# Keys and b/a from the input without its norm factor, with the factor applied at their evacuation; GpSimd makes the sums of squares and the normalized input

## The chip, the cores and the metric

One core of one Trainium2 chip runs the whole program. The metric is the device time of one execution in microseconds, the median of several runs. The engines are TensorE (PE in the profile, with its weight loads as PEld), VectorE (DVE), ScalarE (ACT), GpSimd (POOL) and SyncE (SP, which here only issues DMAs).

## The reference, cut to what matters

Two blocks of a sequence model on 256 positions of width 1024. The change touches only the very beginning, the first layer's input projections:

```python
def rmsnorm(x, w):
    y = x * lax.rsqrt(jnp.mean(x * x, axis=-1, keepdims=True) + EPS)
    return y * w

# gated_deltanet(hn = rmsnorm(x, a_norm_w))
proj = hn @ w_in                                   # 1024 -> q 1024, k 1024, v 2048, z 2048, b 16, a 16
qkv, z, b, a = split(proj)
qkv = silu(causal_dwconv(qkv, conv_w))             # four taps along the positions
q, k = l2norm(q) * 128 ** -0.5, l2norm(k)          # per head
beta, g = sigmoid(b), -exp(a_log) * softplus(a + dt_bias)
o = chunked_gated_delta_rule(q, k, v, g, beta)     # then norm, gate with z, output projection
```

The norm factor is one number per position, so `hn @ w` is `((x * a_norm_w) @ w)` times that factor.
After this layer follow a convolutional MLP, sliding-window attention, a second MLP, and a second block (gated linear attention beside latent attention, and an MLP).

## The kernel before

The activations are held transposed: 8 tiles of 128 channels by 256 positions (`self.h`). Every weight matrix is cut into 128x128 blocks. Eight blocks that are used one after the other lie together as a weight tile of 128x1024 floats (512 KB) in one long array `wall`, in the order of use. `_raw` (line 168) loads a tile through SP's queue. `_prep` (line 175) makes of it a high half `wh` on ScalarE (a copy that rounds, line 186) and a low half `wl` on VectorE (the rest, line 187). Raw tiles and halves have four buffers each. `w` (line 230) hands out the next block and prepares tiles up to two ahead. The input is split in the same way into `xh` and `xl`, and a product is three matmuls (`mm3`, line 247): wh times xh, wh times xl, wl times xh.

`gemm` (line 257) goes over column tiles of the output. With `ko=2` its first four column tiles run together with the channel index k outermost, so that each k needs only one tile of x: this is how Keys start. The others take all eight k for one column tile, one weight tile each.

The program is written in one order, with side tasks that take a step at every fourth block (`side`, `tick`). A scheduler then fixes each engine's own order by the order of writing and by when it reckons operands to be ready; `behind` (line 192) forces one instruction behind another on an engine. At run time each engine executes its list in order and waits with semaphores.

The start (`gdn`, line 547): x is loaded in four quarters ahead of the weights, the identity and the table of small columns. ScalarE squares the quarters, VectorE adds them (line 502) and folds them (line 558), TensorE sums over the channels (`colsum`, line 361), VectorE makes the reciprocal root (`rstd`, `rsqrt_k`, lines 370 and 341), and `rows` (line 410) spreads it over all partitions by a diagonal and a product with ones. Matmuls on ones (`warm`) fill some of the waits. Then for each of the 8 tiles VectorE multiplies x by norm weight and factor (line 568), ScalarE makes `xh` (line 569), VectorE `xl` (line 570).

In `gdn_body` (line 576) Keys' first group runs, then b/a (`w_ba`, evacuated by `evac_ba`, line 605), the rest of Keys, and then Queries, Values and gate z mixed. The evacuation of Keys and Queries is a four-tap convolution (`conv`, line 642): a scaled copy on ScalarE, three multiply-adds on VectorE for each column tile (line 650), a silu, and later sums of squares on TensorE (line 669). Many short-lived tiles share one pool of six buffers (tag `t2`): the normalized x (`xn`), the convolution's `cy`, b/a's `gr` and `gcr`, and others.

## Time and profile before

| | |
|---|---|
| median of 3 runs | 1217.02 us (1215.78 to 1218.51) |
| profiled execution | 1216.23 us, span 1214.4 us |
| TensorE busy | 1188.7 us, 98% |
| VectorE busy | 895.2 us, 74% |
| ScalarE busy | 687.7 us, 57% |
| GpSimd busy | 20.4 us, 2% |
| DMA | 206 MB, 170 GB/s on average |

The profile comes from one execution, on which the times of single instructions rest. Busy is the share of the span in which an engine executes; matmuls are pipelined, so that one of them is recorded longer than the distance to the next. A row of a timeline gives the start, the length, the engine, the line in the program, the operation, what it writes and reads, the shape, and how many like it were merged; in brackets stands how long the engine was idle before it and what released it.

### The profile page before, as it was taken

The page shows a single profiled execution, that of the slowest core. Times are in us where ns is not written, and L with a number is a line of the kernel's source. Part 1 is how long each engine was busy: PE and PEld are TensorE (multiplying, and loading weights), DVE is VectorE, ACT ScalarE, POOL GpSimd, SP SyncE. Part 2 cuts the span into 40 slices and gives each one's busy share as a digit, 9 for nine tenths or more (in the row PEclk, how much of TensorE's full clock was granted, in tenths as well). Part 3 has the DMA queues.
Part 4 walks back from the last instruction along what each step waited for, and adds up shares of the span by engine and source line. Part 5 has one row for each costly group of instructions (what it writes and reads, how often), then busy time and mean ns, then how long its engine had stood idle before and what let it go on. Part 6 is the DMA issues. An engine that isn't in the chain of part 4 may idle for free.

```text
span 1214.4 us, 23416 instructions
## 1 busy us (share of the span) xinstructions
PE 1188.7 (98%) x9368; PEld 1125.4 (93%) x9368; DVE 895.2 (74%) x1680; ACT 687.7 (57%) x1170; POOL 20.4 (2%) x47
## 2 busy tenths in 40 slices
PE   7999989999999999999999999999999999999997
PEld 6989878999999999889999999889789999999996
DVE  6978976668877778878977778756756567655555
ACT  5785547546655556656755556754465445444443
POOL 1000000000000000000000000000000000000000
PEclk9999999999999999999999999999999999999999
DMA  6546365355555557435555564364255563555552
GB/s 222 179 132 216 125 192 183 124 157 168 199 184 182 187 179 243 126 115 161 190 188 183 187 191 158 112 207 134 87 161 173 188 234 118 186 179 187 189 179 83
DMA packets 68318, 206.01 MB, mean 170 GB/s; under 512 B 18198, under 2 KB 18342, under 8 KB 67953
## 3 DMA queue, kind: packets, MB, share of 16 engines
q1 hardware_dynamic: 65600, 194.77, 50.3%
q0 software_dynamic: 2608, 9.75, 2.2%
q8 instruction: 73, 1.20, 0.4%
q14 instruction: 37, 0.29, 0.1%
HBM read 199.75 MB, written 4.74 MB: 168 GB/s over the span
## 4 chain that ended last, share of the span: by engine, by line
PE 92%; DVE 4%; ACT 2%; DMA 1%; issue 1%; SPq 0%; DVEq 0%; ACTq 0%
PE pb L249 21%; PE pb L250 20%; PE pb L251 20%; PE acc L249 7%; PE acc L250 7%; PE acc L251 7%; DVE wl L187 1%; PE pt L1138 1%; PE ssb L669 1%; DMA wr<-wall 0%; DMA h<-xT 0%; PE z2p L855 0%; PE y2p L847 0%; PE kv L1542 0%; PE csum L366 0%
## 5 line engine op out<-in xcount | busy, mean ns | idle before, releaser
L187 DVE TENSOR_TENSOR wl<-wr,wh 128x1024 fp32r<-128x1024 f32 x362 | 441.5, 1223 | 193.7 <-ACT wh L186 192.3
L186 ACT ACTIVATE wh<-wr 128x1024 fp32r<-128x1024 f32 x362 | 381.6, 1057 | 338.3 <-issue 101.1
L251 PE MATMUL pb<-xh,wl 128*128 128x256 f32 x1224 | 345.6, 283 | 3.9 <-DVE wl L187 3.9
L249 PE MATMUL pb<-xh,wh 128*128 128x256 f32 x1224 | 347.8, 284 | 0.6 <-ACT xh L569 0.6
L250 PE MATMUL pb<-xl,wh 128*128 128x256 f32 x1224 | 345.5, 282 | 0.2 <-DVE xl L570 0.2
L249 PEld LDWEIGHTS pb<-xh,wh 128*128 128x128 f32 x1224 | 231.7, 189 | 2.8 <-issue 1.3
L251 PEld LDWEIGHTS pb<-xh,wl 128*128 128x128 f32 x1224 | 229.7, 188 | 4.5 <-DVE wl L187 4.5
L250 PEld LDWEIGHTS pb<-xl,wh 128*128 128x128 f32 x1224 | 230.1, 188 | 0.5 <-DVE xl L570 0.4
L249 PE MATMUL pb<-fh,wh 128*128 128x256 f32 x416 | 118.3, 285 | 0.0
L250 PE MATMUL pb<-fl,wh 128*128 128x256 f32 x416 | 117.5, 283 | 0.1
L251 PE MATMUL pb<-fh,wl 128*128 128x256 f32 x416 | 116.6, 281 | 0.0
L249 PE MATMUL acc<-ah,wh 128*128 128x256 f32 x352 | 98.7, 280 | 0.0
L251 PE MATMUL acc<-ah,wl 128*128 128x256 f32 x352 | 98.5, 280 | 0.0
L250 PE MATMUL acc<-al,wh 128*128 128x256 f32 x352 | 98.5, 280 | 0.0
L249 PEld LDWEIGHTS pb<-fh,wh 128*128 128x128 f32 x416 | 77.9, 188 | 1.4 <-issue 0.4
L250 PEld LDWEIGHTS pb<-fl,wh 128*128 128x128 f32 x416 | 78.1, 188 | 1.1 <-DVE fl L436 0.3
L251 PEld LDWEIGHTS pb<-fh,wl 128*128 128x128 f32 x416 | 78.9, 190 | 0.0
L977 DVE SCALAR_TENSOR_TENSOR fy<-fpad,cols,fy 128x256 f32<-128x256 f32 x176 | 73.6, 478 | 0.0
L249 PE MATMUL pb<-wh,xh 128*128 128x512 f32 (+1 forms) x176 | 70.5, 402 | 0.0
L250 PE MATMUL pb<-wl,xh 128*128 128x512 f32 (+1 forms) x176 | 68.1, 387 | 0.5 <-DVE wl L187 0.5
L251 PE MATMUL pb<-wh,xl 128*128 128x512 f32 (+1 forms) x176 | 68.0, 387 | 0.0
L249 PEld LDWEIGHTS acc<-ah,wh 128*128 128x128 f32 x352 | 66.9, 190 | 0.0
(437 smaller groups left out, 2091.2 us busy)
## 6 DMA issues: line engine op xcount, KB each, us to landing
wr<-wall SPq DMA_DIRECT2D x362, 512.0 KB, 3.6
wzd<-zt POOLq DMA_DIRECT2D x8, 256.0 KB, 3.0
wzog<-wzd POOLq DMA_DIRECT2D x4, 512.0 KB, 5.2
bias<-bd POOLq DMA_DIRECT2D x4, 512.0 KB, 7.7
h<-xT SPq DMA_DIRECT2D x4, 256.0 KB, 4.0
h<-xT POOLq DMA_DIRECT2D x1, 1024.0 KB, 5.9
wrow<-wrow POOLq DMA_DIRECT2D x1, 1024.0 KB, 10.0
out_dram<-mw SPq DMA_DIRECT2D x4, 256.0 KB, 2.0
```

Source lines behind the costliest of these rows:

```text
L186: nc.scalar.activation(hi, r, AF.Copy)
L187: i = nc.vector.tensor_tensor(lo, r, hi.bitcast(F32), ALU.subtract)
L249: mm(out, ah, bh, start=start, stop=False, skip_group_check=skip)
L250: mm(out, ah, bl, start=False, stop=False, skip_group_check=skip)
L251: mm(out, al, bh, start=False, stop=stop, skip_group_check=skip)
L669: nc.tensor.matmul(ssb[:, c : c + 1], sq[:, i, tt * P : tt * P + P], self.ones[:, 0:1], start=True, stop=True)
L977: nc.vector.scalar_tensor_tensor(y[:, i], u[:, i, j : j + T], w(j), y[:, i], ALU.mult, ALU.add)
L1138: nc.tensor.transpose(pt[:, j * P : j * P + P], S[:, i, j * P : j * P + P], self.ident)
```

## The change

x times the norm weight alone is split into `raw` halves, and Keys and b/a are computed from these. Keys' evacuation multiplies by the factor (line 657 of before), and so does that of b/a. The normalized x, which Queries, Values and z still read, is made by a side task on GpSimd and ScalarE. The quarters of x and the first three weight tiles are loaded in turn; the identity goes through GpSimd's queue and the norm weights, by themselves, through ScalarE's. The first conversions stand in a written order on ScalarE and VectorE. Two of the additions of squares and one half of the folding move to GpSimd. In the k-outer products all wh times xh of one k come first, then wh times xl, then wl times xh. Three small products on VectorE are forced behind other work.

```diff
-WARM = (5, 1, 3)
+WARM = 16
+NA1, NA2 = 4, 2
@@ gemm, ko
             for k in range(K):
+                ts = []
                 for g in range(ko):
                     for i, c in enumerate(groups[g]):
-                        wh, wl = self.w(name, k * P, c * P)
-                        self.mm3(banks[g][:, i * T : i * T + T], wh, wl, xh[:, k], xl[:, k],
-                                 k == 0 and i == 0, k == K - 1, True)
+                        ts.append((banks[g][:, i * T : i * T + T], *self.w(name, k * P, c * P), k == 0 and i == 0))
+                mm = self.nc.tensor.matmul
+                for o, wh, wl, first in ts:
+                    mm(o, wh, xh[:, k], start=first, stop=False, skip_group_check=True)
+                for o, wh, wl, first in ts:
+                    mm(o, wh, xl[:, k], start=False, stop=False, skip_group_check=True)
+                for o, wh, wl, first in ts:
+                    mm(o, wl, xh[:, k], start=False, stop=k == K - 1, skip_group_check=True)
@@ run
+            self.ones = self.cp.tile([P, P], F32, name="ones")
+            nc.gpsimd.memset(self.ones, 1.0)
+            self.anw = self.cp.tile([P, KD], F32, name="anw")
+            nc.scalar.dma_start(self.anw, self.a["cols"][:, 0:KD])
             for b in range(4):
                 nc.sync.dma_start(self.h[:, 2 * b : 2 * b + 2], self.a["xT"][:, 2 * b : 2 * b + 2])
-            nc.sync.dma_start(self.ident, self.cst("ident"))
-            self._raw(0)
+                if b < 3:
+                    self._raw(b)
+            nc.gpsimd.dma_start(self.ident, self.cst("ident"))
             nc.sync.dma_start(self.cols, self.a["cols"])
@@ gdn (all of the old chain goes)
-            warm(WARM[0], self.ones)
-            for b in range(4):
-                self.add_sq(self.sqs, "sqa", b, lambda o: nc.scalar.activation(o, self.h[:, 2 * b : 2 * b + 2], AF.Square))
-            nc.vector.tensor_tensor(self.sqs[0], self.sqs[0], self.sqs[1], ALU.add)
-            cs = self.colsum(self.sqs[:1])
...
-            rc = self.rstd(cs, D)
...
-            rb = self.rows(rc, psum=True)
...
-            for i in range(8):
-                t = gp.tile([P, T], F32, tag="t2", bufs=6, name="xn")
-                op = nc.vector.scalar_tensor_tensor(t, self.h[:, i], self.col("a_norm", i), rb, ALU.mult, ALU.mult)
-                nc.scalar.activation(x[0][:, i], t, AF.Copy)
-                nc.vector.tensor_tensor(x[1][:, i], t, x[0][:, i].bitcast(F32), ALU.subtract)
...
+            for _ in range(WARM):
+                nc.tensor.matmul(wb[:, 0:P], self.ones, self.ones, start=True, stop=True)
+            raw = (gp.tile([P, KD, T], F32R, tag="XA", name="rawh"), gp.tile([P, KD, T], F32R, tag="EA", name="rawl"))
...
+            def rawtile(i):
+                act.append(nc.scalar.activation(raw[0][:, i], self.h[:, i], AF.Copy, scale=self.anw[:, i : i + 1]))
+                dve.append(nc.vector.scalar_tensor_tensor(raw[1][:, i], self.h[:, i], self.anw[:, i : i + 1], raw[0][:, i].bitcast(F32), ALU.mult, ALU.subtract))
+            def part(j, s):
+                r, hi, lo = self.raws0[j], *self.halves[j]
+                act.append(nc.scalar.activation(hi[:, s], r[:, s], AF.Copy))
+                dve.append(nc.vector.tensor_tensor(lo[:, s], r[:, s], hi[:, s].bitcast(F32), ALU.subtract))
+            def square(b):
+                t = gp.tile([P, 2, T], F32, tag="t2", bufs=6, name="sq")
+                act.append(nc.scalar.activation(t, self.h[:, 2 * b : 2 * b + 2], AF.Square))
+                return t
...
+            rawtile(0)
+            part(0, lo)
+            rawtile(1)
+            part(0, hi)
+            rawtile(2)
+            rawtile(3)
+            part(1, full)
+            s0 = square(0)
+            rawtile(4)
+            rawtile(5)
+            s1_ = square(1)
+            self._raw(3)
+            nc.gpsimd.tensor_tensor(s0, s0, s1_, ALU.add)
+            part(2, full)
+            s2_ = square(2)
+            nc.gpsimd.tensor_tensor(s0, s0, s2_, ALU.add)
+            rawtile(6)
+            rawtile(7)
+            s3_ = square(3)
+            self._raw(4)
+            nc.gpsimd.tensor_tensor(s0[:, 0], s0[:, 0], s0[:, 1], ALU.add)
+            dve.append(nc.vector.tensor_tensor(s3_[:, 0], s3_[:, 0], s3_[:, 1], ALU.add))
+            for l in (act, dve):
+                for p, n in zip(l, l[1:]):
+                    self.behind(n, p)
...
+            def norm():
+                for _ in range(NA1):
+                    yield
+                rc = self.rstd(self.colsum([s0[:, 0], s3_[:, 0]]), D)
+                for _ in range(NA2):
+                    yield
+                self.rb = self.rows(rc)
+                self.ready = True
+                self.flush()
+                for i in range(8):
+                    t = gp.tile([P, T], F32, tag="t2", bufs=6, name="xn")
+                    nc.gpsimd.tensor_tensor(t, self.ha[i], self.rb, ALU.mult)
+                    nc.scalar.activation(x[0][:, i], t, AF.Copy)
+                    nc.gpsimd.tensor_tensor(x[1][:, i], t, x[0][:, i].bitcast(F32), ALU.subtract)
+                    yield
...
+            for i in range(8):
+                nc.gpsimd.tensor_tensor(self.ha[i], self.h[:, i], self.anw[:, i : i + 1].to_broadcast([P, T]), ALU.mult)
+            self.side(norm())
@@ evac_ba
-            nc.vector.tensor_scalar(xa[A], b[A, :T], ...)
+            nc.vector.tensor_tensor(e1[A], b[A, :T], self.rb[A], ALU.mult)
+            nc.vector.tensor_scalar(xa[A], e1[A], ...)
@@ mk_evac
+                if key == "kss":
+                    u = t2([P, 2, T], "ku")
+                    nc.vector.tensor_tensor(u, ev2(b), self.bc2(self.rb), ALU.mult)
+                    b = u.rearrange("p a t -> p (a t)")
                 conv(b, ct0 + 2 * g, d)
@@ Keys and b/a
-        gk = self.gemm("w_in", x, KD, list(range(8, 16)), mk_evac(kT, 0, 8, "kss"), ko=2)
+        gk = self.gemm("w_in", raw, KD, list(range(8, 16)), mk_evac(kT, 0, 8, "kss"), ko=2)
         next(gk)
-        list(self.gemm("w_ba", x, KD, [0], evac_ba))
+        list(self.gemm("w_ba", raw, KD, [0], evac_ba))
@@ identr, and in ffn the two products wfp and w1f
+            self.behind(nc.vector.tensor_tensor(...), ...)
```

## Rows read from the trace of the kernel before

**Rows 1.** The page's busy time by engine: us, share of the span, instructions.
```profile
PE 1188.7 (98%) x9368; PEld 1125.4 (93%) x9368; DVE 895.2 (74%) x1680; ACT 687.7 (57%) x1170; POOL 20.4 (2%) x47
```
**Rows 2.** Busy time by stretches; first the view's own column names.
```profile
core 0: us, PE busy (x) PEld busy (x) DVE busy (x) ACT busy (x) POOL busy (x), PEclk, DMA share, GB/s
0.00:15.00 15.00, 7.46 (x26) 5.68 (x26) 6.71 (x25) 7.62 (x11) 1.36 (x9) 1.00 0.75 269
...
28.00:40.00 12.00, 12.00 (x102) 12.00 (x101) 10.99 (x24) 10.55 (x17) 0.00 (x0) 1.00 0.62 209
40.00:52.00 12.00, 12.00 (x104) 12.00 (x103) 11.94 (x22) 8.59 (x13) 0.00 (x0) 1.00 0.45 140
...
240.00:480.00 240.00, 239.84 (x2004) 238.41 (x2003) 192.27 (x322) 140.35 (x223) 4.79 (x10) 1.00 0.57 182
```
**Rows 3.** Timeline of TensorE, first 16 us; a matmul of f32 is recorded as two.
```profile
0.99 2.50 PE L554 MATMUL warm<-ones 128*128 128x128 f32 x10 [0.99 <-POOL ones L524]
9.29 1.01 PE L366 MATMUL csum<-ones,sqa 128*128 128x1 f32 x4 [5.80 <-DVE sqa L558]
15.02 0.50 PE L249 MATMUL pb<-xh,wh 128*128 128x256 f32 x2 [0.59 <-ACT xh L569]
```
**Rows 4.** Timeline of ScalarE, 4 to 62 us.
```profile
4.11 0.63 ACT L557 ACTIVATE sqa<-h 128x512 f32<-128x512 f32 x1 [2.10 <-DMA h<-xT]
...
8.43 1.06 ACT L186 ACTIVATE wh<-wr 128x1024 fp32r<-128x1024 f32 x1 [1.23 <-DMA wr<-wall]
...
10.45 1.06 ACT L186 ACTIVATE wh<-wr 128x1024 fp32r<-128x1024 f32 x1 [0.74 <-DMA wr<-wall]
...
16.22 1.01 ACT L569 ACTIVATE xh<-xn 128x256 fp32r<-128x256 f32 x3
...
28.62 0.46 ACT L647 ACTIVATE cy<-pb,cols 128x256 f32<-128x256 f32 x1
...
50.23 1.06 ACT L186 ACTIVATE wh<-wr 128x1024 fp32r<-128x1024 f32 x1 [0.85 <-PE pb L250]
```
**Rows 5.** Timeline of TensorE, two matmuls in a row and a block of sums.
```profile
24.06 0.28 PE L250 MATMUL pb<-xl,wh 128*128 128x256 f32 x1
24.18 0.28 PE L251 MATMUL pb<-xh,wl 128*128 128x256 f32 x1
...
46.01 0.95 PE L669 MATMUL ssb<-ones,sqg 128*128 128x1 f32 x8
```
**Rows 6.** Timeline of VectorE, 5 to 49 us; merged rows overlap a little.
```profile
5.81 0.69 DVE L502 TENSOR_TENSOR sqa<-sqa,sq 128x512 f32<-128x512 f32 x1 [5.81 <-ACT sq L557]
...
10.34 0.16 DVE L379 TENSOR_SCALAR rv<-csum 128x2 f32<-128x2 f32 x1 [1.11 <-PE csum L366]
...
12.93 0.48 DVE L416 TENSOR_SCALAR dg<-ident,rd 128x128 f32<-128x128 f32 x2
...
15.22 0.75 DVE L570 TENSOR_TENSOR xl<-xn,xh 128x256 fp32r<-128x256 f32 x2
...
18.82 1.26 DVE L568 SCALAR_TENSOR_TENSOR xn<-h,cols,rowp 128x256 f32<-128x256 f32 x3
...
28.75 1.23 DVE L187 TENSOR_TENSOR wl<-wr,wh 128x1024 fp32r<-128x1024 f32 x1 [2.52 <-ACT wh L186]
...
41.47 2.43 DVE L650 SCALAR_TENSOR_TENSOR cy<-pb,cols,cy 128x255 f32<-128x255 f32 x6
...
47.13 1.21 DVE L187 TENSOR_TENSOR wl<-wr,wh 128x1024 fp32r<-128x1024 f32 x1
```
**Rows 7.** A cast on GpSimd, VectorE beside it; line 187's shortest, median, longest in ns.
```profile
21.08 0.66 POOL L588 CAST mask3b<-mask 128x384 bf16<-128x384 f32 x1
...
21.31 1.52 DVE L187 TENSOR_TENSOR wl<-wr,wh 128x1024 fp32r<-128x1024 f32 x1
...
L187 DVE TENSOR_TENSOR wl<-wr,wh x362: 1202/1225/1520, 10.7 to 1198.2; 128x1024 fp32r<-128x1024 f32 x181
```

More of the change, by code (lines that the diff above doesn't have):

```diff
@@ new lines, in part @@
+            def part(j, s):
[6 more added lines that the diff above has]
+                return t
+            self.raws0 = {}
@@ new lines, in gdn @@
+            for j in range(3):
+                self.raws0[j] = self.raws.pop(j)
+                self.raws[j] = None
+                self.halves[j] = (self.wtile(j, F32R, "wh"), self.wtile(j, F32R, "wl"))
+            lo, hi, full = slice(0, 512), slice(512, 1024), slice(0, 1024)
+            rawtile(0)
[7 more added lines that the diff above has]
+            rawtile(4)
@@ L577, in gdn_body @@
+            hab = gp.tile([P, KD, T], F32, tag="vn", name="ha")
+            self.ha = [hab[:, i] for i in range(8)]
+            for i in range(8):
+                nc.gpsimd.tensor_tensor(self.ha[i], self.h[:, i], self.anw[:, i : i + 1].to_broadcast([P, T]), ALU.mult)
+            self.side(norm())
+            self.gdn_body(gp, x, raw)
+    def gdn_body(self, gp, x, raw):
         nc, tc, sp = self.nc, self.tc, self.sp
```

28 lines of the change are left out of this document (9 added, 19 removed).

## The prediction

> **What bounds the kernel now.** I read the page first [rows 1]: TensorE (PE) is busy 98% of the span, VectorE (DVE) 74%, GpSimd (POOL) 2%. The table by stretches [rows 2] then says where the missing 2% lie: PE is busy all of the long middle stretch, 239.84 of 240 us, and only 7.46 us of the first 15. So a start-up change can win at most the idle part of those 15 us, and only if PE still has its inputs afterwards. The timelines of the start come next. PE waits 5.80 us for the sums of squares, then for the chain behind them (sum over partitions, reciprocal root, row broadcast), and the first real product starts at 15.02 us [rows 3]. Nothing in Keys' product needs that factor before its result is normalized: that is what the change uses.
>
> The reader must see a second thing before adding up a gain. From 28 to 52 us, while PE is full, DVE is busy 10.99 and 11.94 of 12 us [rows 2]. It makes the low halves of the weights there (wl, line 187) and evacuates Keys. A faster start of PE is worth only what DVE can follow.
>
> **Where the two engines stand.** One matmul follows another by 0.12 us [rows 5], so a weight tile (8 blocks of 3 matmuls) is 24 x 0.12 = 2.88 us. Number the weight tiles: 0 to 3 are Keys' first four column tiles, 4 is b/a, 5 to 8 the rest of Keys, 9 and on are Queries. ScalarE's conversion of tile 14 waits at 50.23 for the slot that tile 10 gives back [rows 4], so PE begins tile 11 at about 50.3. Two blocks of sums (0.8 us each, [rows 5]) and a small transpose lie in between, so tile 9 began at 50.3 - 2 x 2.88 - 0.8 = 43.7 and tile 4 at 50.3 - 7 x 2.88 - 1.8 = 28.3; the first evacuation of Keys at 28.62 [rows 4] agrees. DVE ends the wl of tile 11 at 48.3 [rows 6], 2.0 us ahead of PE.
>
> **The change, part by part.** *Loads.* x no longer goes ahead of all weights; its quarters alternate with weight tiles. x's first quarter (0.26 MB) was usable at 4.11 and weight 0, behind 1.64 MB in all, at 8.43 [rows 4]: 1.38 MB in 4.3 us, 318 KB per us. After the change weight 0 ends at 0.79 MB: 4.11 + 0.52/0.318 = 5.8. Weight 1 (1.57 MB) comes at 8.2, weight 2 (2.36 MB) between 10.2 and the 10.45 of weight 1 before. The small load of norm weights goes by ScalarE's queue, which had nothing to do until 4.11; the identity moves to POOL's queue, from which nothing before the row broadcast waits. Both I cost at nothing; if the norm weights came late, all of x's conversion would move with them, one for one.
>
> *Conversions.* ScalarE's order is now fixed. From 5.8 it does weight 0 in halves (2 x 0.6), seven x tiles (0.34 each, three in 1.01 [rows 4]), weights 1 and 2 (1.06 each) and four squares (0.63): 1.2 + 2.4 + 2.1 + 2.5 = 8.2, to 14.0. DVE trails by one add: 14.9. Weight 3's high half ends at 15.2, its low half at 16.4, and PE has 12 matmuls behind that: 17.9, plus 1.0 for the column sums [rows 3], which stand in PE's queue and hold the products behind them: 18.9. PE then begins tile 4 at 18.9 against 28.3: a lead of **9.4 us**. The 16 warm-up matmuls cost 0.5 each by their row [rows 3], so to 9.0 at worst, ahead of the first product at 6.6. From 9.0 the four tiles take 4 x 2.88 + 1.0 = 12.5, to 21.5; that bound shortens the lead to 6.8 and is still not what comes last below.
>
> *DVE behind it.* Between 15.0 and 48.3 DVE worked 33.3 - 2.5 idle = 30.8 us [rows 6]. Out of this the normalized x goes (8 x 0.42 and 8 x 0.38 = 6.4) and two wl that now lie in the start-up (2.4). In come the reciprocal root (10.34 to 12.93 less one wl = 1.4), the diagonal (0.5), the factor on 3.3 of Keys' four evacuations (0.69 each, priced by a 128x512 add: 2.3) and on b/a (0.4). Keys' convolution now reads SBUF instead of PSUM; I take 0.03 off each of 20 steps (0.405 against 0.375 [rows 6]), 0.6. Sum: 30.8 - 6.4 - 2.4 + 4.6 - 0.6 = 26.0, and tile 11's wl would end at 14.9 + 26.0 = **40.9**. PE could be at tile 11 at 50.3 - 9.4 = 40.9 too. If nothing else happened, all 9.4 us would stay.
>
> *POOL.* It gets 8 products with the norm weights and 3 adds in the start-up, and 16 operations (a product and a subtraction for each of 8 tiles) that make x for Queries. No row shows a two-input operation on POOL. The nearest is the cast of 128x384 at 0.66 us [rows 7], which moves 384 elements in and 384 out; 512 in and 256 out is as much, so I take 0.66, with 0.48 and 0.96 (by elements in alone, once and twice 256) as ends.
>
> What does POOL do to DVE? In [rows 7] that cast lies from 21.08 to 21.74, and the wl that starts inside it at 21.31 takes 1.52 us, the longest of all 362, where the median is 1.225. So one POOL operation cost one DVE operation 0.30 us, by one pair of rows. The Trainium skill (SBUF — State Buffer, Who interferes with whom) states that a DVE instruction with two SBUF inputs and a GpSimd instruction that reads SBUF block each other for a whole instruction; the trace agrees in kind, with 0.30 of 0.43 us of overlap. The 16 operations fall from 21.4 on, where DVE does wl and convolution without a break, and through the change the convolution has both inputs in SBUF as well. I take 16 x 0.30 = **4.8 us** on DVE, with 0 and 16 x 0.66 = 10.6 as ends. The 11 operations of the start-up fall where DVE waits for data for some 3 us; at 0.30 each they are 3.3, so I cost them at nothing, and 3.3 is the end of that range.
>
> *x for Queries.* The column sums end at 15.9, root and up to two wl ahead of it at 19.7, broadcast and copy at 21.4. POOL's 16 operations then need 10.6: 32.0. Tile 9 would begin at 43.7 - 4.6 = 39.1 and use its last x at 41.6, so POOL has room for (41.6 - 21.4)/16 - 0.66 = 0.6 us of waiting on each: no cost taken.
>
> *Rest.* The order of matmuls in the k-outer products (high times high first) changes no count; PE is full at these places [rows 2], so nothing. The three orderings that keep two tiny products off the start-up save or cost 0.2 us; nothing.
>
> **The sum.** Tile 11 begins at 40.9 + 4.8 = 45.7 instead of 50.3: **4.6 us** earlier, and behind it the work is the same. The profiled execution took 1216.23 us (span 1214.4, 1.8 around it): 1211.6. It lies 0.8 below the median, so in the median's terms 1217.02 - 4.6 = **1212.4**.
>
> **Rivals.**
> 1. *POOL does not hold DVE*, or only where DVE waits anyway. For it: DVE's single-SBUF-input steps, and only one pair of rows shows a hold. Against it: the longest wl of all is just that one. Gain 9.4: 1207.6.
> 2. *POOL holds DVE for each whole operation.* 40.9 + 10.6 = 51.5 against 50.3: 1.2 slower, 1218.2, no change that can be told. It takes away the gain from 9.4/16 = 0.59 us of hold per operation. For it: the stated rule, and DVE's nearly full stretch. Against it: 0.30 was measured. The skill's page GPSIMD Engine Reference (Engine selection) also advises VectorE for elementwise work; on DVE these 16 would cost 6.4 us, so with it the gain would be 3.0 and the move is worth 1.6 by my sum.
> 3. *x comes late* (the slower side). The hold works both ways: a POOL operation waits out the DVE operation under way, and each product, conversion and subtraction is a chain over two engines; x also shares six buffers (tag t2) with Keys' and b/a evacuations, which now overlap it. If each of the 16 waits for one wl (1.2 us), x is complete at 21.4 + 16 x 1.86 = 51.2, where Queries' tile 9 used its last x at 43.7 + 2.5 = 46.2: 5.0 slower, 1222.0. It is slower than before from a wait of (46.2 - 21.4)/16 - 0.66 = 0.89 each.
> 4. *The change does not do what it says*: a program's scheduler puts the column sums so early that PE stands before them. They can't run before 14.9; tiles 2 and 3 behind them then end at 15.9 + 5.8 = 21.7. The lead is 6.6, still above 4.6: it is in the forecast's range.
>
> **How the numbers follow.** Forecast with its surroundings (gain 2.4 to 7): 0.43. Rival 1: 0.15. Rival 2, with all between -2.4 and 2.4: 0.25. Rival 3: 0.17. A change of 0.2% (2.4 us) is about what a measurement of this kernel can tell. Faster 0.58, same 0.25, slower 0.17. The range goes from rival 1, 1207.5, to 1220.0, which holds rival 2 with the start-up's hold and the smaller half of rival 3; the forecast's own range is 1210.0 to 1214.6.
>
> **What would show it.** The first product at 6.5 to 9 us, tile 4 (b/a) at 19 to 22, not 28. wl's longer than 1.225 beside POOL operations, 0.3 each. PE waiting for wl (line 187) between 20 and 50, little for x; if PE's longest wait there is for xl from POOL, it is rival 3. I am wrong on the size if POOL's operations take well over 1 us, and wrong in kind if the lead at tile 4 isn't there.

## The result, and the profile after

The changed kernel takes 1233.31 us (median of 4 runs, 1233.21 to 1234.05) against 1216.84 us for the kernel before on the same chip: a ratio of 1.0136, 95% interval 1.0120 to 1.0152, or 16.5 us slower. Forecast were 1212.4 us, a range of 1207.5 to 1220.0, and slower with a chance of 0.17. The time lies outside the range, on the side that had the least chance.

The profiled execution has a span of 1231.5 us. Its busy time by engine answers to [rows 1]:

```profile
PE 1197.6 (97%) x9386; PEld 1135.4 (92%) x9386; DVE 903.1 (73%) x1675; ACT 696.5 (57%) x1185; POOL 45.7 (4%) x75
```

The table by stretches, to be held against [rows 2]:

```profile
core 0: us, PE busy (x) PEld busy (x) DVE busy (x) ACT busy (x) POOL busy (x), PEclk, DMA share, GB/s
0.00:15.00 15.00, 12.84 (x87) 12.59 (x87) 8.03 (x12) 10.84 (x20) 6.40 (x15) 1.00 0.85 308
15.00:28.00 13.00, 9.51 (x51) 9.51 (x52) 8.29 (x21) 3.30 (x4) 7.58 (x11) 0.61 0.39 128
28.00:40.00 12.00, 12.00 (x103) 12.00 (x102) 11.29 (x14) 7.53 (x14) 10.25 (x10) 1.00 0.48 154
40.00:52.00 12.00, 3.71 (x23) 3.54 (x23) 9.05 (x18) 8.47 (x13) 4.60 (x6) 0.64 0.08 30
```

The stretch from 15 to 28 us before the change, in the same columns:

```profile
15.00:28.00 13.00, 12.11 (x96) 11.71 (x97) 11.23 (x19) 5.62 (x11) 2.25 (x3) 1.00 0.45 148
```

The start is as wanted: 12.84 us of work in the first 15 instead of 7.46. The next 13 us give it back, and from 40 to 52 us, where TensorE was full before, it works 3.71 us. The granted clock is 0.61 and 0.64 in these two stretches (1.00 before). The timeline of TensorE after the change shows where:

```profile
6.85 0.73 PE L270 MATMUL pb<-rawh,wh 128*128 128x256 f32 x4
...
12.83 0.64 PE L270 MATMUL pb<-rawh,wh 128*128 128x256 f32 x4
13.31 0.52 PE L272 MATMUL pb<-rawl,wh 128*128 128x256 f32 x3
18.49 0.59 PE L372 MATMUL csum<-ones,sq 128*128 128x1 f32 x2 [4.67 <-POOL sq L610]
...
22.29 1.05 PE L272 MATMUL pb<-rawl,wh 128*128 128x256 f32 x4
...
28.23 0.36 PE L248 MATMUL pb<-rawh,wh 128*128 128x256 f32 x1
...
49.59 0.50 PE L702 MATMUL bgp<-ident,stk 80*128 80x80 f32 x2 [8.29 <-issue]
```

Line 270 is Keys' first product, line 372 the column sums, line 248 at 28.23 b/a (tile 4 of the prediction's count), line 702 the small transpose of b/a. The first product starts at 6.85 (15.02 before, [rows 3]) and runs without a gap to 13.8. Then the column sums wait 4.67 us for GpSimd. The matmuls behind them come at 1.05 us for four where four took 0.64 (12.83), at the lower of the clock's two levels (granted 0.50, below). So b/a starts at 28.2, where it started before, and the lead of 9.4 us is gone. Then the transpose of b/a waits another 8.29 us (the view names no releaser for it; see below).

**An account of the loss.** The beginning of the first MLP (its column sums) lies at 285.2 us before and at 301.3 after; of the 17.1 us between the two profiled executions 16.1 arise ahead of it. TensorE's busy time up to there, before and after:

```profile
0.00:285.20 285.20, 271.33 (x2329) 1.00 0.52 169
```
```profile
0.00:301.30 301.30, 279.45 (x2340) 0.95 0.49 160
```

That is 13.9 us idle before, 21.8 after. The busy time is 8.1 us longer with the same products. The stretches of after, 5 us each, in which the clock was low and TensorE busy:

```profile
core 0: us, PE busy (x), PEclk, DMA share, GB/s
15.00:20.00 5.00, 1.51 (x7) 0.60 0.28 98
20.00:25.00 5.00, 5.00 (x25) 0.50 0.24 63
25.00:30.00 5.00, 5.00 (x40) 0.87 0.84 281
50.00:55.00 5.00, 5.00 (x25) 0.50 0.11 18
55.00:60.00 5.00, 5.00 (x35) 0.80 0.56 192
90.00:95.00 5.00, 4.58 (x21) 0.66 0.58 133
```

Busy time times what the clock lacks of 1.00 is 0.6 + 2.5 + 0.65 + 2.5 + 1.0 + 1.55 = 8.8 us; over all such stretches it is 9.2. This is a little high: four matmuls come every 0.85 us at a granted clock of 0.50 (22.29 to 23.14) and every 0.48 at 1.00 (12.83 to 13.31), 1.77 times as long and not twice. So the change lost some 8 us to idle time and some 8 to the half clock (1.2 instead of 2.4 GHz). Work at full clock, with the 9.2 taken off, is 271.3 us before and 279.45 - 9.2 = 270.2 after; in the profiles of the ten variants below that add nothing to TensorE's work, it lies between 270.2 and 272.6. Each of these sums is of one execution, the profiled one. They make a kernel's start readable in two numbers, to a microsecond or two.

**GpSimd and VectorE.** The timeline of GpSimd:

```profile
12.68 3.10 POOL L638 TENSOR_TENSOR ha<-h,anw 128x256 f32<-128x256 f32 x3
15.74 1.44 POOL L605 TENSOR_TENSOR sq<-sq 128x512 f32<-128x512 f32 x1
...
17.72 0.71 POOL L610 TENSOR_TENSOR sq<-sq 128x256 f32<-128x256 f32 x1
...
28.98 1.43 POOL L629 TENSOR_TENSOR xn<-ha,rowb 128x256 f32<-128x256 f32 x2 [5.22 <-ACT rowb L428]
...
47.68 1.52 POOL L631 TENSOR_TENSOR xl<-xn,xh 128x256 fp32r<-128x256 f32 x2
```

Three products with the norm weights stand ahead of the second sum, which they hold to 15.74. The factor arrives at 28.9 (forecast 21.4), x is complete at 49.2 (forecast 32.0). Beside GpSimd's operations VectorE slows down:

```profile
29.88 1.62 DVE L186 TENSOR_TENSOR wl<-wr,wh 128x1024 fp32r<-128x1024 f32 x1 [0.19 <-ACT wh L185]
31.42 5.35 DVE L717 SCALAR_TENSOR_TENSOR cy<-ku,cols,cy 128x255 f32<-128x255 f32 x6
...
38.17 0.83 DVE L678 TENSOR_SCALAR gr<-gr,cols 48x256 f32<-48x256 f32 x1
...
46.37 1.62 DVE L690 TENSOR_TENSOR_SCAN gcr<-ones,gr 16x128 f32<-16x128 f32 x2
...
49.21 0.28 DVE L694 TENSOR_SCALAR stk<-gcr 16x256 f32<-16x256 f32 x1
49.41 0.34 DVE L692 CAST gch<-gcr 16x384 fp32r<-16x384 f32 x1
```

Six steps of Keys' convolution take 5.35 us (2.43 before, [rows 6]); b/a's evacuation runs from 36.7 to 49.8. The transpose reads `stk`, whose last write (line 694) ends at 49.49; TensorE starts it at 49.59.

### The profile page after: what moved, and what is told of

It reads as the page before. It is cut to its first block, busy times and chain, and to the rows that moved or that the text cites. A ratio compares the mean times of both kernels' runs of the same rounds, so it can differ in the third digit from the quotient of the medians.

```text
span 1231.5 us, 23493 instructions
## 1 busy us (share of the span) xinstructions
PE 1197.6 (97%) x9386; PEld 1135.4 (92%) x9386; DVE 903.1 (73%) x1675; ACT 696.5 (57%) x1185; POOL 45.7 (4%) x75
## 4 chain that ended last, share of the span: by engine, by line
PE 90%; DVE 4%; ACT 2%; issue 1%; DMA 1%; POOL 0%; DVEq 0%; SPq 0%; ACTq 0%
PE pb L248 19%; PE pb L249 19%; PE pb L250 19%; PE acc L248 7%; PE acc L250 7%; PE acc L249 7%; PE pb L274 1%; PE pb L272 1%; PE pb L270 1%; DVE wl L186 1%; DMA wr<-wall 1%; PE ssb L740 1%; DVE cy L717 1%; PE pt L1209 1%; ACT wh L185 0%
## 5 line engine op out<-in xcount | busy, mean ns | idle before, releaser
L248 PE MATMUL pb<-xh,wh 128*128 128x256 f32 x1072 | 306.0, 285 | 1.8 <-ACT wh L185 1.8
L250 PE MATMUL pb<-xh,wl 128*128 128x256 f32 x1072 | 304.2, 284 | 3.2 <-DVE wl L186 3.2
L249 PE MATMUL pb<-xl,wh 128*128 128x256 f32 x1072 | 303.3, 283 | 0.0
L248 PEld LDWEIGHTS pb<-xh,wh 128*128 128x128 f32 x1072 | 204.1, 190 | 3.7 <-ACT wh L185 1.9
L250 PEld LDWEIGHTS pb<-xh,wl 128*128 128x128 f32 x1072 | 202.1, 189 | 3.6 <-DVE wl L186 3.6
L249 PEld LDWEIGHTS pb<-xl,wh 128*128 128x128 f32 x1072 | 202.6, 189 | 0.1
```

What stands on the lines that cost most here:

```text
L248: mm(out, ah, bh, start=start, stop=False, skip_group_check=skip)
L249: mm(out, ah, bl, start=False, stop=False, skip_group_check=skip)
L250: mm(out, al, bh, start=False, stop=stop, skip_group_check=skip)
```

## The experiments

All kernels but that of the second point are made from the changed one, those of points 3 and 4 with the edits of e3 besides; differences are told as ratios to the kernel before on the same chip, times 1217 us.

**Theories.** A (the hold theory of the recorded texts): GpSimd's operations hold VectorE more than was priced. B (the queue theory): the sums come late, in GpSimd's queue, and everything follows from that wait. C (the evacuation theory): the added factor step on Keys and b/a is what can't be hidden. D: the half clock behind the new waits is a cost of its own.

**1. Who makes x and the sums.** Four kernels: x for Queries back on VectorE, and the eight products with the norm weights gone with it; only the three sums on VectorE; both; and GpSimd's products forced behind its sums.

```diff
 e1, e3:
-            for i in range(8):
-                nc.gpsimd.tensor_tensor(self.ha[i], self.h[:, i], ...anw..., ALU.mult)
-                    nc.gpsimd.tensor_tensor(t, self.ha[i], self.rb, ALU.mult)
+                    nc.vector.scalar_tensor_tensor(t, self.h[:, i], self.anw[:, i : i + 1], self.rb, ALU.mult, ALU.mult)
-                    nc.gpsimd.tensor_tensor(x[1][:, i], t, ..., ALU.subtract)
+                    nc.vector.tensor_tensor(x[1][:, i], t, ..., ALU.subtract)
 e2, e3 (three times):
-            nc.gpsimd.tensor_tensor(s0, s0, s1_, ALU.add)
+            dve.append(nc.vector.tensor_tensor(s0, s0, s1_, ALU.add))
 e4:
+                self.behind(<product ha[i] on GpSimd>, <third sum on GpSimd>)
```

> The changed kernel, but VectorE makes the normalized x (a product with norm weight and factor, and the subtraction, as before the change), and the eight products of x with the norm weight on GpSimd are gone; GpSimd keeps the three additions of the sums of squares. If GpSimd's operations hold VectorE's and VectorE's hold GpSimd's (the hold theory), the convolution steps of Keys fall from 0.89 us each to 0.4, the two long waits of TensorE (4.7 us for the sums, 8.3 us ahead of b/a's transposes) shrink to under 2 each, and the time is 1212 to 1219 us. If the late factor and the heavier evacuations of Keys and b/a are the cause (the evacuation theory), the 6.4 us that VectorE gets in addition make it worse: the 8.3 us wait stays or grows and the time is 1231 us or more. If only the column sums in TensorE's queue and the clock behind that wait matter (the queue theory), the 4.7 us wait goes because the products ahead of the sums are gone, the 8.3 us wait stays, and the time is 1223 to 1227 us.

> The changed kernel, but VectorE does the three additions of squares that GpSimd did; GpSimd still makes the products with the norm weight and the normalized x. Hold theory: the 4.7 us wait for the sums shrinks to about 2 us, the wait ahead of b/a's transposes stays at 7 us or more, since x and the evacuations still meet; time 1225 to 1230 us. Queue theory: the first wait and the half clock behind it go, 8 us in all; time 1223 to 1226 us with the second wait as it was. Evacuation theory: the factor comes some 4 us earlier and the second wait shrinks by as much; 1224 to 1228 us.

> The changed kernel with no arithmetic of GpSimd left in the start: VectorE makes the normalized x and the three additions. Hold theory: both long waits are gone and the lead of TensorE at the b/a product (9 us) survives in part; 1208 to 1215 us, faster than before the change. Evacuation theory: VectorE has some 9 us more to do until Queries begin, so the second wait stays; 1225 us or more. Queue theory: as with the sums alone on VectorE, 1223 to 1226 us.

> The changed kernel with one thing forced: GpSimd's eight products with the norm weight stand behind its three additions of squares. Queue theory: TensorE's wait for the sums falls from 4.7 us to under 2.5, its clock stays up, and the time falls by 5 to 8 us, to 1225 to 1228. Hold theory: the wait falls too, but what TensorE wins there is lost again in front of b/a's transposes, where the wait grows from 8.3 to 11 us or more; time 1230 to 1234 us.

| kernel | us (before on that chip) | ratio, interval | us over before | longest waits of TensorE at sums, broadcasts and the transpose, up to 240 us |
|---|---|---|---|---|
| changed | 1233.31 (1216.84) | 1.0136 [1.0120, 1.0152] | 16.5 | b/a 8.3, sums 4.7 |
| e1, x on VectorE | 1226.31 (1218.61) | 1.0067 [1.0043, 1.0091] | 8.2 | Keys' sums 3.6, column sums 2.1, b/a 2.0 |
| e2, sums on VectorE | 1230.11 (1218.61) | 1.0088 [1.0059, 1.0117] | 10.7 | b/a 6.4, row broadcast 2.1 |
| e3, both | 1222.99 (1218.61) | 1.0032 [1.0012, 1.0051] | 3.9 | Keys' sums 3.4, row broadcast 1.9, b/a 1.8 |
| e4, products behind sums | 1231.57 (1218.61) | 1.0105 [1.0076, 1.0134] | 12.8 | b/a 8.8, column sums 1.7 |

x on GpSimd costs 8.3 us with the sums there (changed to e1) and 6.8 without (e2 to e3); the sums cost 5.8 and 4.3. These are differences of ratios whose intervals reach 1.5 to 3.5 us to either side. B alone falls with e4: the wait for the sums goes from 4.7 to 1.7, and the wait for b/a is still 8.8. The times of e1 and e3 lie where B had put them, and 7 to 8 us above the forecasts of A; what speaks for A is the wait for b/a, which B leaves as it is and which falls to 2.0 and 1.8, and the lengths of VectorE's steps. A holds: in e3, without two-input operations on GpSimd, the same steps of VectorE take their short times and b/a's evacuation ends at 38.7 instead of 49.8, 5.6 us of which are the factor's earlier arrival (23.3 instead of 28.9). VectorE in e3:

```profile
25.45 2.45 DVE L713 SCALAR_TENSOR_TENSOR cy<-ku,cols,cy 128x255 f32<-128x255 f32 x6
...
30.07 0.40 DVE L674 TENSOR_SCALAR gr<-gr,cols 48x256 f32<-48x256 f32 x1
...
36.97 0.73 DVE L686 TENSOR_TENSOR_SCAN gcr<-ones,gr 16x128 f32<-16x128 f32 x2
...
38.38 0.34 DVE L688 CAST gch<-gcr 16x384 fp32r<-16x384 f32 x1
```

**2. The price of a GpSimd operation beside VectorE.** The kernel before, with 60 products, 60 copies and 60 memsets of 128x256 added on GpSimd in the first MLP, where TensorE waits for nothing.

```diff
+            if layer == 0:      # one generator beside the MLP, two operations at each step
+                60 x nc.gpsimd.tensor_tensor(pc, pa, pb, ALU.mult)
+                60 x nc.gpsimd.tensor_copy(pc, pa)
+                60 x nc.gpsimd.memset(pc, 1.0)
```

> The kernel before, with 180 operations of GpSimd on tiles of its own (128x256, f32) added to the first MLP: first 60 products of two tiles, then 60 copies, then 60 memsets, two at a side step. They belong to nothing. Hold theory: where one lies beside an operation of VectorE with two inputs from SBUF (the low half of a weight, the convolution's steps), that one takes 0.3 to 0.5 us longer than its median, and GpSimd's product takes 0.9 us instead of 0.6; the memsets, which read nothing, hold nobody. If the longer convolution steps of the changed kernel have another cause, low halves and convolution steps keep their lengths of 1.22 and 0.48 us. TensorE is fully busy there, so the time changes by less than 5 us either way.

1234.53 us (a single time), 16.8 more than before; less than 5 were expected. VectorE's lines 187 (wl, two inputs in SBUF), 996 (convolution, two in SBUF) and 989 (one in PSUM, one in SBUF), shortest, median and longest in ns; first beside the products, then the copies, then the memsets:

```profile
L187 DVE TENSOR_TENSOR wl<-wr,wh x15: 1207/1744/1761, 278.4 to 340.3; 128x1024 fp32r<-128x1024 f32 x15
L996 DVE SCALAR_TENSOR_TENSOR fy<-fpad,cols,fy x23: 471/952/961, 301.4 to 343.2; 128x256 f32<-128x256 f32 x23
L989 DVE TENSOR_TENSOR fpad<-pb,rowb x6: 675/678/679, 299.6 to 339.7; 128x512 f32<-128x512 f32 x6
...
L187 DVE TENSOR_TENSOR wl<-wr,wh x16: 1274/1364/1415, 344.6 to 386.7; 128x1024 fp32r<-128x1024 f32 x16
L996 DVE SCALAR_TENSOR_TENSOR fy<-fpad,cols,fy x22: 611/612/961, 343.2 to 386.2; 128x256 f32<-128x256 f32 x22
...
L187 DVE TENSOR_TENSOR wl<-wr,wh x8: 1214/1216/1227, 389.9 to 406.6; 128x1024 fp32r<-128x1024 f32 x8
L996 DVE SCALAR_TENSOR_TENSOR fy<-fpad,cols,fy x12: 475/476/480, 392.8 to 408.9; 128x256 f32<-128x256 f32 x12
```

Beside products one VectorE operation loses 0.48 to 0.52 us, beside copies 0.14, beside memsets nothing; and the operation with an input in PSUM loses nothing at all. The products themselves take 0.80 us in the median (0.72 to 1.73). The waits of TensorE over this stretch, of which the kernel before has none:

```profile
PE pb L251 <- DVE wl L187: 5.1, 2, 3.1
PE acc L251 <- DVE wl L187: 3.9, 2, 2.4
PE rowp L418 <- DVE dg L416: 2.3, 1, 2.3
```

So the hold alone, with no wait for GpSimd's results, makes TensorE wait. All of it lies beside the products: from 279 to 344 us TensorE is idle for 11.7 us and its granted clock is 0.92, and beside the copies and memsets (344 to 409) it is full, at 1.00.

**3. The added factor step.** e3 without the multiplication of Keys by the factor.

```diff
-                if key == "kss":
-                    u = t2([P, 2, T], "ku")
-                    nc.vector.tensor_tensor(u, ev2(b), self.bc2(self.rb), ALU.mult)
-                    b = u.rearrange("p a t -> p (a t)")
```

> No GpSimd arithmetic in the start, and Keys' evacuation leaves the factor out (Keys are then not normalized by it, so part of the computation is missing): four operations of VectorE less, the convolution reads from PSUM again, and it needn't wait for the factor. If the added step and its wait are what makes the evacuations late, the second sums' wait of 3.4 us goes, the fourth evacuation of Keys ends by 56 us, and the time falls by 4 us or more, to 1215 to 1219. If the normalized x, which now shares VectorE and ScalarE with the evacuations instead of going ahead of them, is what makes them late, the time falls by less than 2.5 us.

1215.78 us against 1218.18, ratio 0.9977 [0.9964, 0.9990]: 2.8 us faster than before and 6.7 less than e3. C holds: four operations of 0.68 us, 2.7 us of VectorE time, cost 6.7. Keys' second squares, for which TensorE waits 3.4 us in e3, come late behind this step, b/a's evacuation and x; in e10 that wait isn't among TensorE's waits at all, and 9.6 instead of 15.0 us are idle up to the first MLP. e10 takes away three things at once: the step's time on VectorE, Keys' wait for the factor, and the step's place in the pool of six buffers; how the 6.7 us divide among them wasn't tested. With the step for nothing, and all else as in e3, the change gives 2.8 us.

**4. Moving the waiting products.** If TensorE only meets these waits too early, later places should free it: Keys' sums and the transpose some steps later (e6), also the first quarter of z from the input without its factor (e7), this alone (e11), and this with x eight steps later (e9). e5 gives the later k-outer products their old order of matmuls, for a difference of 1.0 us in each MLP's stretch.

```diff
 e5:  +   if name != "w_in": <three matmuls of one weight in a row, as before>
 e6:  -   for _ in range(WSSB): yield        +   15 steps for Keys (9 before)
      -   for _ in range(6): yield           +   10 (ahead of b/a's transpose)
 e7, e9, e11:
      -   gz = self.gemm_nat("w_in", x, KD, [4096, 4608, 5120, 5632], 512, evac_z)
      +   <columns 4096 from raw, the factor as the evacuation's scale; the rest from x>
 e9:  +   for _ in range(8): yield           ahead of x for Queries
```

> The kernel without GpSimd arithmetic in the start (the one before, in which VectorE makes sums and normalized x), with the old order of matmuls (high times high, high times low, low times high, one block after the other) in the k-outer products of both MLPs and of the attention; only the first product keeps the new order. From the column sums of one norm to those of the next, every kernel with the new order takes 193.3 us for the first MLP where the kernel before takes 192.3, and 205.2 against 204.1 for the second with what follows, and 84.2 against 85.2 for the attention. If the order of matmuls makes these, the three stretches go back to 192.3, 85.2 and 204.1 and the time falls by 1 us; if they come from elsewhere (the scheduler's other lists), they stay.

> The kernel without GpSimd arithmetic in the start, in which TensorE's sums of squares for Keys stand 15 side steps behind their evacuation instead of 9, and b/a's transposes 10 instead of 6. If TensorE's lead (9 us at the b/a product) is lost only because these small matmuls stand in its queue ahead of products that could run (the queue theory), its waits of 3.4 and 1.8 us there go, the half clock behind them too, and the time falls by 5 us or more, to 1216 to 1218. If VectorE and ScalarE simply have too much to do between the factor and the first product of Queries (the evacuation theory), TensorE waits for x or the weights' low halves instead, and the time stays within 2 us of 1223.

> As the one with the sums later, and besides the first quarter of z is computed right behind Keys, from the input without the factor (its rows are positions there, so ScalarE's copy of the result takes the factor as a scale and costs nothing more); x is then needed 11.5 us later. Evacuation theory: the start's lead survives in good part, no wait over 2 us until Queries begin, and the time is 1208 to 1215 us, below the kernel before. Queue theory: as with the sums later alone, no gain beyond 2 us from this. If the loss after 60 us (a wait of 1.8 us for a weight's high half and the half clock behind it, 3.5 us in all) is independent of the start, it is still there and the time is 1213 to 1216.

> No GpSimd arithmetic in the start; the first quarter of z is computed behind Keys from the input without the factor (which ScalarE's copy of the result then applies as a scale), and the normalized x is made eight side steps later, so that the evacuations of Keys and b/a have VectorE to themselves in between. Sums and transposes stand where they do in the changed kernel. If what comes last is the evacuation of Keys (the fourth ends at 59.1 us without GpSimd arithmetic against 56.2 before the change, and the first product of keys with keys follows), it now ends at 52 to 56, TensorE's wait for the second sums (3.4 us) goes, and the time is 1213 to 1219 us. If the time hangs on TensorE's own queue and the scheduler's lists instead, the fourth evacuation moves but the time stays above 1222.

> As the one with the first z behind Keys, but the normalized x is made where the changed kernel makes it, among the evacuations. Against the one with x made later it tells what x costs the evacuations: if x is the burden, the wait for the second sums stays at 3 us or more, the fourth evacuation of Keys ends 3 us or more later, and the time is 3 us or more above that one's. If the place of z alone decides, the two times agree within 1.5 us.

| kernel | us (before on that chip) | ratio, interval |
|---|---|---|
| e5, old order in later products | 1224.56 (1217.73) | 1.0055 [1.0037, 1.0072] |
| e6, sums and transpose later | 1232.94 (1217.73) | 1.0110 [1.0081, 1.0139] |
| e7, e6 with z first | 1240.08 (1217.73) | 1.0168 [1.0131, 1.0204] |
| e11, z first | 1224.13 (1218.18) | 1.0046 [1.0034, 1.0058] |
| e9, z first, x later | 1224.87 (1218.18) | 1.0058 [1.0042, 1.0075] |

None gains on e3. Forecasts of 1208 to 1219 us for e6, e7 and e9 were missed. Against e3, e6 and e7 lose 10 and 17 us: steps beside the products are counted in TensorE's work, and Keys' products with themselves, which every later stage needs, start at 71.0 and 71.3 us (62.6 in e3). e9 and e11 idle less than before (12.5 and 13.3 us) and lose 9.0 and 5.4 us at the half clock, in their profiled executions. Their times agree, so x's place doesn't decide between them. e5's stretches are unchanged, so the order of matmuls isn't the cause of the 1.0 us; that cause stays open.

**5. The half clock.** TensorE's waits filled with products of ones by ones that nothing reads, placed directly ahead of the product that waits.

```diff
+    def fill(self, out, n, p):          # into an unused part of the waiting product's bank
+        for _ in range(n):
+            self.behind(self.nc.tensor.matmul(out, self.ones, self.ones, start=True, stop=True, ...), p)
 e12 (changed kernel):  12 ahead of the column sums, 22 ahead of b/a's transpose
 e16 (changed kernel):  18 and 35
 e13 (e3), e14 (e11), e15 (e9):  5 ahead of the row broadcast, 2 to 4 ahead of the transpose, 2 to 9 ahead of Keys' sums
```

> The changed kernel with TensorE's two long waits filled: 12 products of ones by ones (0.35 us each by the 32 records of the start-up, 5.6 us) stand directly ahead of the column sums, into an unused part of their bank, and 22 directly ahead of b/a's small transpose; they are 4.2 of the 4.7 us wait and 7.7 of the 8.3 us wait, and nothing reads them. Everything else is as in the changed kernel. Up to the first MLP's column sums the changed kernel's TensorE was idle 21.8 us (13.9 before) and lost 9.2 us of work at the half granted clock (none before), and idle plus loss make up the 16.1 us by which it stands there later. Theory (the half clock is the consequence of these waits, and costs): windows 15 to 30 and 45 to 60 us show a granted clock of 1.00, some 7.5 of the 9.2 us come back, time 1225 to 1227. Rival (the clock falls for another reason, or TensorE isn't what waits last): no change, 1232 to 1234. A third case, filled products that themselves delay the sums: 1235.

> The kernel with sums and x on VectorE (1223.0 us), its three waits filled in the same way: 5 products of ones ahead of the row broadcast (wait 1.9 us), 4 ahead of b/a's transpose (1.8), 9 ahead of Keys' second sums (3.4). There TensorE lost 5.1 us to the half clock up to the first MLP, 3.7 of them from 40 to 52 us and 1.4 from 82 to 88. Theory: the 3.7 come back, 1219.0 to 1220.0, still not below the kernel before (idle 15.0 against 13.9). Rival: 1223.

> The kernel that makes the first quarter of z from the input without its factor (1224.1 us; idle 13.3, lost clock 5.4 up to the first MLP), waits filled: 5 products ahead of the row broadcast, 2 ahead of b/a's transpose, 9 ahead of Keys' second sums. The half clock stands at 22 to 27 (1.5 us lost), 43 to 50 (2.5) and 145 to 150 (1.5, not filled). Theory: 4.0 come back, 1220. Rival: 1224.

> The same with x for Queries later (1224.9 us; idle 12.5, the least of the exact variants, but 9.0 us lost at the half clock): 5 products ahead of the row broadcast, 4 ahead of b/a's transpose, 2 ahead of Keys' second sums. The half clock stands at 38 to 52 us (6.6 us lost), 92 to 98 (1.7) and 147 to 153 (1.6). Theory: it goes from 38 to 52 and 6 to 6.6 us come back, 1218 to 1219, level with the kernel before. If TensorE runs out of inputs the sooner for being faster, half of it is lost again: 1221.5. Rival (the clock is no cause): 1225.

> The changed kernel again with its two waits filled, now by the products' own duration: 24 records of the first filling took 2.84 us, 0.24 us a product and not 0.35, so 3.3 us of each wait were left and the clock still fell behind them. Now 18 products (4.3 us) ahead of the column sums and 35 (8.3 us) ahead of b/a's transpose. If the half clock is the consequence of the waits, it is gone from 15 to 27 and from 48 to 60 us. If it is then also what costs there, some 7 of the 9.2 us come back: 1226. If VectorE's work (conversions, Keys, b/a) sets the pace and TensorE only waits longer, the clock is full there and the time stays at the 1230 of the first filling.

| kernel | us (before on that chip) | ratio, interval | its base | lost clock, base to filled (profiled executions) | granted clock over a whole run, median of all runs, base to filled |
|---|---|---|---|---|---|
| e12 | 1230.29 (1217.15) | 1.0106 [1.0084, 1.0128] | 1.0136 | 9.2 to 7.7 us | 0.986 to 0.991 |
| e13 | 1224.73 (1217.15) | 1.0064 [1.0049, 1.0079] | 1.0032 | 5.1 to 3.0 | 0.992 to 0.9925 |
| e14 | 1222.38 (1217.15) | 1.0044 [1.0026, 1.0061] | 1.0046 | 5.4 to 6.7 | 0.990 to 0.9915 |
| e15 | 1222.74 (1217.15) | 1.0049 [1.0032, 1.0066] | 1.0058 | 9.0 to 4.6 | 0.9905 to 0.993 |
| e16 | 1228.09 (1216.47) | 1.0090 [1.0073, 1.0107] | 1.0136 | 9.2 to 4.6 | 0.986 to 0.996 |

The first filling was too short: a product took 0.24 us, not 0.35, so in e12 waits of 3.3 us for the sums and 3.4 for b/a stayed. e16 fills b/a's wait whole, and the clock there is full, where the changed kernel had 0.64 and then 0.50:

```profile
42.61 7.98 PE L254 MATMUL bgp<-ones 128*128 128x128 f32 x70
...
50.42 0.30 PE L709 MATMUL bgp<-ident,stk 80*128 80x80 f32 x2
```

The stretches there, in the columns of the first table:

```profile
40.00:52.00 12.00, 12.00 (x108) 12.00 (x107) 9.06 (x18) 8.63 (x14) 4.63 (x6) 1.00 0.09 34
52.00:60.00 8.00, 7.94 (x67) 7.73 (x66) 7.17 (x13) 4.88 (x8) 0.00 (x0) 1.00 0.53 161
```

Work that nothing reads made the changed kernel faster, by 5.6 us in ratios; the intervals of e16 and of the changed kernel lie apart. The account agrees: e16's first MLP begins at 296.8 instead of 301.3 us; idle time (11.4 us) and filling (12.1) together are no less there than the 21.8 us of idle time in the changed kernel; what is less is the lost clock, 4.6 for 9.2. With the filling the scheduler also changed some places in the order of VectorE and ScalarE, and the column sums come 2 us later (20.6), so the filling isn't the only difference. D holds in part: the half clock is a consequence of the long waits and costs by itself. It is not the whole: 11 us remain.

For the short waits D isn't shown. In the two profiled executions e13 regains 2.1 us of clock, but those were the slowest run of e3 and the fastest of e13; over all runs the clock is nearly the same, and the time is if anything worse (1.0064 against 1.0032). TensorE waits 5.3 us there for wl instead of 3.2. e14 and e15 have a little more clock over all their runs, and their times agree with their bases' within the intervals.

## Why the prediction was wrong

The steps that failed are the terms for GpSimd's work (x at 4.8 us of hold, the sums at nothing) and for the factor step on Keys (1.7 us), and two that the sum didn't have: the evacuation of b/a from end to end, for which TensorE waits, and the clock behind such waits.

**What held.** The first product was forecast for 6.6 and came at 6.85; the loads carried it. The lead was there until 13.8 us. With x and the sums on VectorE and the factor step left out (e10), the kernel is 2.8 us faster. The prediction's own terms say 4.7 for that: 4.6, less 1.6 for x's move, plus 1.7 for the step on Keys (2.3, less 0.6 for the convolution).

**The miss by terms.** From 4.6 us faster to 16.5 slower are 21.1 us. The measured terms depend on the order in which the edits are taken back, and the two smallest lie within the intervals:

| step of the prediction | it took | measured | miss, us |
|---|---|---|---|
| x on GpSimd rather than VectorE | 1.6 us gain (4.8 hold against 6.4) | 6.8 us loss (e2 to e3) | 8.4 |
| sums on GpSimd | nothing (at most 3.3, with the eight products) | 4.3 (e1 to e3) | 4.3 |
| x and sums together | nothing | 12.6 less 6.8 and 4.3 | 1.5 |
| factor step on Keys | 1.7, by VectorE's sum | 6.7 (e10 to e3) | 5.0 |
| the rest of the start-up's lead | 4.7 us gain | 2.8 (e10) | 1.9 |

**The hold: a size, from one pair of rows.** 0.30 us an operation was read from a cast on GpSimd [rows 7], the only row that showed anything. A cast reads one input; the change's operations read two, and beside those a VectorE operation loses 0.48 to 0.52 (e8). The rule that the prediction weighed, from the Trainium skill (SBUF — State Buffer, Who interferes with whom), is that the one blocks the other for a whole instruction. The trace agrees in kind, as 0.30 did, and less in size: 0.52 on a wl of 1.22 us and 0.476 on a step of 0.476 are less than GpSimd's product takes, 0.80 in the median of e8 and 0.60 at the shortest in the changed kernel. Rival 2 was built on it and put the break-even at 0.59 us an operation. With 0.52 the sum would still have had 9.4 - 16 x 0.52 = 1.1 us of gain, so the price alone doesn't make the loss. The hold goes both ways, which stood in rival 3 and not in the sum: GpSimd's operations, taken at 0.66, took 0.94 to 0.97 on the mean. And it falls on other steps than wl and convolution: beside GpSimd's operations b/a's scaling, with one tensor read from SBUF, takes 0.83 (0.40 in e3), its scan, with two, 1.62 for 0.73, and these stand in the chain for which TensorE waits.

**The start-up's operations on GpSimd, taken at nothing.** The prediction asked what they do to VectorE, and not what stands ahead of the sums in GpSimd's own queue, though rival 4 came near it: there TensorE stood before the sums until 14.9, and a lead of 6.6 was left. In fact GpSimd's sums ended at 18.4, since three products of 1.03 us, one of 0.60 and a sum of 1.44 (0.69 on VectorE, [rows 6]) lay ahead of the last. The lead at b/a was then nothing, as the test named in the prediction's last part says: wrong in kind if the lead at tile 4 isn't there.

**The clock.** No term for it stood in the sum. In the profile of before, the 13.9 us of idle time cost no clock: the granted clock is 1.00 in every stretch up to the first MLP. After, each of the two long waits is followed by some 8 us at or near the half clock. To 8 us more of idle time come some 8 lost in clock; filling the waits brings 5.6 us back in e16.

**The factor step.** VectorE's time was summed, and 0.6 us taken off because the convolution reads SBUF: the steps take 0.477 us from SBUF and 0.473 from PSUM, so nothing came off. What was missing is that the step is one more link in Keys' chain (factor, step, convolution, squares, sums), behind a factor which comes later than Keys' first product ends (23.3 against 20.3 us in e3). The reader sees it in e3's wait of 3.4 us for Keys' squares, and in its absence in e10.

**The chain of b/a, and ScalarE in it.** The prediction followed TensorE's lead through VectorE's summed time and had no term for the time b/a's evacuation takes from end to end. Before, it ran from 32.3 to 39.6, and the transpose waited for nothing; one function-table load of ScalarE stands in it:

```profile
32.33 0.53 DVE L611 TENSOR_SCALAR gr<-pb,cols 48x256 f32<-48x256 f32 x1
...
34.13 1.28 ACT L617 ACT_TABLE_LOAD   x1
...
39.26 0.34 DVE L625 CAST gch<-gcr 16x384 fp32r<-16x384 f32 x1
...
40.62 0.30 PE L635 MATMUL bgp<-ident,stk 80*128 80x80 f32 x2
```

After the change two stand in it, behind a silu of Keys that now comes first:

```profile
39.99 1.28 ACT L682 ACT_TABLE_LOAD   x1
...
42.11 1.28 ACT L684 ACT_TABLE_LOAD   x1
```

That is 7.3 us before, 13.1 in the changed kernel, and still 10.1 in e3 (28.6 to 38.7), which has the two loads as well. So e3, in which b/a begins at 22.7 on TensorE, 5.6 us ahead of before, gets past the transpose only 1.9 us ahead. What the second load costs wasn't tested.

**Small slips.** By the prediction's own rate weight 2 (2.36 MB) comes at 10.7 us, not between 10.2 and 10.45, and the ends for GpSimd's operation by elements in alone are 0.44 and 0.88, not 0.48 and 0.96. Nothing in the sum hangs on either.

**The rivals.** Rival 3, x late, is the nearest: x was complete at 49.2 us (its worst case said 51.2), and slower was its sign. But its mechanism, a wait for x at Queries, isn't what ended last. TensorE stood ahead of that at b/a's transpose, and e4, which shortens the way to x, gives 3.7 of 16.5 us.

**What stays open.** From Keys' products with themselves to the first MLP the changed kernel, e1 to e4, e6 and e10 need 229 to 231 us, the kernel before 226.2. In the changed kernel, with 229.8, most of the 3.6 us have a place: a wait for a weight's high half, which ScalarE makes, and 1.6 us of half clock behind it (90 to 95 us, above).

```profile
90.42 0.39 PE L248 MATMUL pb<-xh,wh 128*128 128x256 f32 x1 [1.77 <-ACT wh L185]
```

Between 71.5 and 82 us ScalarE loads function tables five times there, for three times in the same work before (59.9 to 68.3); that this makes the high half late is likely and wasn't tested. In the profiled execution of e10, which idles 4.3 us less than before up to the first MLP, 4.7 us of lost clock use that up, and the first MLP begins at 285.1, no earlier than before. But it was the slowest of e10's eight runs (1218.5 us, granted clock 0.991, the others 0.993 to 0.996), so no trace shows where the 2.8 us of the median come from; nor do the runs say why its short waits cost clock and the longer ones of before don't. In the changed kernel, e3 and e5 the first MLP's stretch takes 193.3 us and 192.3 before, the attention's 84.2 and 85.2, the next 205.2 and 204.1; the order of matmuls isn't the cause (e5), and another wasn't found.

## What to carry to other kernels

A wait that a change removes at the head of TensorE's queue is worth only what the next waiting products leave of it: list each product in that queue that waits for another engine (sums, transposes, broadcasts) and date it anew, before adding up any gain. Elementwise work moved to GpSimd is paid by VectorE, at half a microsecond for each two-input operation of 128x256 here, in both directions; where VectorE is nearly full, as here, that work cost more there than on VectorE itself (6.8 to 8.3 us for x). Split a start-up's difference into idle time and work at the half clock, as above: the two numbers together must give the shift, to a microsecond or so. A long wait that can't be removed may be worth filling (5.6 us came back with the 8.3 us wait filled and part of the other); filling waits of 1 to 3 us gained nothing that could be told here. Take such an account from more than one execution where the runs of a kernel differ in granted clock.

## What the runs showed of the hardware

An operation of GpSimd with two inputs adds 0.52 us to a VectorE subtraction of 128x1024 (1.22 to 1.74) and doubles a convolution step (0.476 to 0.952); a copy adds 0.14; a memset adds nothing; a VectorE operation of 128x512 with one of its two inputs in PSUM stays at 0.68 beside all of them (e8). A function-table load of ScalarE takes 1.28 us. TensorE's granted clock fell to 0.50 behind waits of 4.7 and 8.3 us in the changed kernel and stayed there for several microseconds of full work; with the second wait filled it stayed at 1.00. It did not fall in every case: in e3 it stayed at 1.00 behind a wait of 1.9 us at 22, and in e10, behind a wait of the same length at the same place, it was 0.69 and 0.62 in the next 5 us.
